# Fifteen shared up-projection blocks instead of thirteen, with four of their gates made in the mixer

## The chip, the core and the metric

One core of a Trainium2 chip runs the whole program. The metric is the device time of one execution in microseconds (us). TensorE (PE) does the matrix products, VectorE (DVE), ScalarE (ACT) and GpSimd (POOL) the elementwise work, and SyncE (SP) issues the transfers between DRAM and the on-chip memory. Each engine takes its instructions in a fixed order and waits at the head of that order for what the next one needs. Results of PE land in eight banks of accumulator memory (PSUM), each 128 x 512 fp32.

## What is computed

One decoder layer on 1024 tokens of width 1024: a mixer (RWKV-7 heads beside a causal convolution, one input and one output projection) and then a gated feed-forward part of hidden width 2816. The change touches the second:

```
h   = rms_norm(x, norm_pre_ffn)
hid = h @ ffn_up                      # 1024 -> 2 x 2816
hid = causal_dwconv(hid, width 3) + b
f   = (gelu(hid[:, :2816]) * hid[:, 2816:]) @ ffn_down
x   = x + rms_norm(f, norm_post_ffn)
```

## The kernel before

**Tiles.** The 1024 tokens are two halves, h0 and h1, of 512. The 2816 hidden columns are FT = 22 blocks of 128; block i has a gate (branch 0) and an up part (branch 1). Every fp32 factor is split into a high and a low part, so one product of a 128x128 weight tile with 512 tokens is three matmuls (high·high, high·low, low·high). One branch of one block for one half is 8 weight tiles, so 24 matmuls of 512 columns, in two weight loads of four tiles each; `weight` loads 256 KB, ACT casts the high part (`wh`) and POOL or DVE subtracts for the low part (`wl`).

**Two ways for a block.** `ffn_pair` makes both branches of one block for one half: 48 matmuls, 96 for both halves. The other way saves products by a Strassen scheme over (two halves of the tokens) x (gate, up) x (two halves of the 1024 inputs): `gates` makes the full gate of h0, which is 24 matmuls, and keeps the partial product after the first four weight tiles (`firsts`); later `shared` gets everything else out of five products of 12 matmuls, from sums of weights (`four_sums`) and sums of activations (`act_sums`). That is 84 matmuls. JOINT blocks go the second way, PLAIN = FT - JOINT the first.

**Order.** The mixer comes first. In its last part PE alternates between the small matmuls of the recurrence, of `conv_norm` and of the other chains, and `ffn_pair` of h0 for the first EARLY blocks, whose results go to DRAM (`early`). The mixer has only two banks, tag `pb`, for these products: each new product takes the bank of the product before the last one and has to wait until `taps` has read that. `taps` is one pass of ACT over the bank, a small ACT copy of two columns, and two passes of DVE (L910, L912, L919). `w_out` for h1 ends the mixer. Then come `gates` for the shared blocks, `ffn_pair` of h1 for the plain ones (with `act_sums` and `weight_sums` interleaved by `beside`), `shared`, and `ffn_down`, a Strassen scheme again, whose weight sums `weight_sums` has left in DRAM (12 sets: four 256 KB loads, four POOL operations, four 256 KB stores each). In the feed-forward part products rotate over six banks. The order of instructions on each engine is set by a scheduler from priorities when the program is built.

In the order of the code before, EARLY = 9, JOINT = 13, PLAIN = 9.

Of the kernel before, what the change touches and what calls it, by code (L numbers as in the profile page):

```python
# [52 lines left out]
EARLY = 9  # L53

JOINT = 13
PLAIN = FT - JOINT

# [43 lines left out]
class Trunk:  # L101
# [99 lines left out]
    def setup(self):  # L201
# [23 lines left out]
        self.lows = self.dp.tile([22, 2, P, 4, P], F32, name="lows")  # L225
        self.sums = self.dp.tile([4, HT, P, 512], F32, name="sums")
# [551 lines left out]
    def w_out(self, h, mixr, co, behind=None):  # L778
# [13 lines left out]

        def evac(ch, pss, post):
# [15 lines left out]
        for ch in range(4):  # L809
# [3 lines left out]
            for k2 in range(KT // 2):  # L813
                wh, wl = self.weight(self.a["w_out"][ch, k2], [P, 2, 256], (self.mix, "ca", "ck") if h else None)
                if ch == 1 and k2 == 0:
                    mark = self.load
# [15 lines left out]
        return mark  # L832


    def setup_ffn(self, ctx):
# [14 lines left out]
                      **{t: cycle([self.wq] * MORE_PAIRS + [self.wp] * PAIRS) for t in ("wh", "wl")}}  # L850
        self.post_ffn = cp.tile([P, D], F32, name="post_ffn")
# [51 lines left out]
    def taps(self, h, i, br, ps, acc):  # L903
# [3 lines left out]
        carry = (self.ecarry if i < EARLY else self.fcarry)[:, br, i]  # L907
# [13 lines left out]
    def ffn_pair(self, h, hs, i, temp, out=None):  # L921
# [10 lines left out]
        self.gated = nc.vector.tensor_tensor(out, gate, accs[1], ALU.mult)  # L932
        return out
# [25 lines left out]
    def gates(self, hs, acts, firsts, side):  # L959
# [9 lines left out]
        for n, i in enumerate(range(PLAIN, FT)):  # L969
# [118 lines left out]
    def weight_sums(self):  # L1088

        nc, a = self.nc, self.a  # L1090
        work = [(lambda r, c, j=j: a["ffn_down"][c, r * HT + j], lambda n, j=j: self.sums[n - 1, j]) for j in range(HT)]
        work.insert(2, (lambda r, c: a["ffn_up"][c * FT + PLAIN, r].rearrange("p k m -> p (k m)"),
                        lambda n: self.usums[n - 1]))
        for src, dst in work:
            b = [self.tp.tile([P, 512], F32, tag="tp", name=self.nm("b")) for _ in range(4)]
# [27 lines left out]
    def ffn_down(self, acts):  # L1123
# [4 lines left out]
        B = lambda r, c: lambda j: self.a["ffn_down"][c, r * HT + j]  # L1128
# [92 lines left out]
    def run(self):  # L1221
# [6 lines left out]
        with ExitStack() as ctx:  # L1228
# [5 lines left out]
            sums = self.weight_sums()  # L1234
            temp = lambda: self.f2p.tile([P, HALF], F32, tag="f2", name=self.nm("acc"))
            act = lambda: self.ap.tile([P, HALF], F32, tag="act", name=self.nm("act"))
            one = [self.ffn_pair(0, h0, i, temp, act()) for i in range(EARLY, PLAIN)]
            both = [[act() for _ in range(JOINT)] for _ in range(2)]
            turn = cycle((True, False))
            self.gates(h0, *both, lambda: self.beside(*[norm] if len(h1) == 0 else [norm, sums] if next(turn) else []))  # L1240
# [9 lines left out]
            for n, i in enumerate(range(PLAIN, FT)):  # L1250
                self.shared(i, S, h1[4:], both[0][n], both[1][n], raws[n % 2 * 4:n % 2 * 4 + 4] if n else None)
            kept = []
            for i in range(0, 8, 2):
# [234 lines left out]
```

## Time and profile before

| | |
|---|---|
| three runs | 1252.01, 1254.13 (median), 1255.34 us |
| the profiled execution | 1257.58 us, of which the span of the profile is 1255.8 us |
| mean granted clock of PE | 0.985 |
| busy, share of the span | DVE 72%, ACT 58%, POOL 40% |
| mixer up to the first up-projection of h0 | 0 to 500 us |
| mixer, recurrence beside early blocks | 500 to 640 us |
| `w_out` for h1 | 640 to 698 us |
| feed-forward part | 698 us to the end; the last matmuls end about 9 us before it (row at 1243.76 us, twelve matmuls in 2.88 us) |

A row of a timeline or of a list of groups gives engine, line of the code, operation, output, input and shape. The duration of a matmul in it runs from its issue to its modelled end, and successive matmuls overlap; so the time that a stream of matmuls takes is read from the distance of their starts, not from the mean duration.

### The profile page before, as it was taken

The page shows a single profiled execution, that of the slowest core. Times are in us where ns is not written, and L with a number is a line of the kernel's source. Part 1 is how long each engine was busy: PE and PEld are TensorE (multiplying, and loading weights), DVE is VectorE, ACT ScalarE, POOL GpSimd, SP SyncE. Part 2 cuts the span into 40 slices and gives each one's busy share as a digit, 9 for nine tenths or more (in the row PEclk, how much of TensorE's full clock was granted, in tenths as well). Part 3 has the DMA queues.
Part 4 walks back from the last instruction along what each step waited for, and adds up shares of the span by engine and source line. Part 5 has one row for each costly group of instructions (what it writes and reads, how often), then busy time and mean ns, then how long its engine had stood idle before and what let it go on. Part 6 is the DMA issues. An engine that isn't in the chain of part 4 may idle for free.

```text
span 1255.8 us, 22979 instructions
## 1 busy us (share of the span) xinstructions
PE 1210.4 (96%) x8424; PEld 988.9 (79%) x8424; DVE 899.8 (72%) x1558; ACT 729.1 (58%) x1515; POOL 507.1 (40%) x447
## 2 busy tenths in 40 slices
PE   5999999999999998999999999999999999999997
PEld 4767777787778876778889888888888888888885
DVE  5285998898669989998640555666656679479667
ACT  7563564565955676466762576876555566554451
POOL 4343330001103331344563399998888850000002
PEclk9999998999999989999999999999999999999999
DMA  7644442333343353222364798894322335336413
GB/s 243 177 131 137 129 135 64 97 128 119 114 128 91 97 178 110 75 80 85 104 186 118 271 323 293 298 315 153 82 74 81 101 134 166 95 117 219 134 52 134
DMA packets 102912, 180.97 MB, mean 144 GB/s; under 512 B 14896, under 2 KB 21424, under 8 KB 102800
## 3 DMA queue, kind: packets, MB, share of 16 engines
q1 hardware_dynamic: 102800, 179.51, 45.6%
q8 instruction: 66, 1.08, 0.4%
q14 instruction: 46, 0.38, 0.1%
HBM read 138.44 MB, written 41.03 MB: 143 GB/s over the span
## 4 chain that ended last, share of the span: by engine, by line
PE 62%; DVE 6%; ACT 2%; issue 1%; DMA 1%; POOL 1%; POOLq 0%; DVEq 0%; ACTq 0%
PE pb L140 27%; PE xs L140 16%; PE pe L140 14%; PE Y L140 2%; PE pc L140 2%; DVE pc L431 2%; DMA pt<-mixd 1%; PE pc L155 1%; PE pe L155 0%; DVE x L1120 0%; DVE m L167 0%; DVE sub L606 0%; DVE nrow L1136 0%; DVE dw L608 0%; DVE t L797 0%
## 5 line engine op out<-in xcount | busy, mean ns | idle before, releaser
L167 POOL TENSOR_TENSOR wl<-wr,wh 128x512 fp32r<-128x512 f32 (+1 forms) x175 | 230.0, 1316 | 219.4 <-ACT wh L167 191.3
L140 PE MATMUL pb<-h,wh 128*128 128x512 f32 (+3 forms) x720 | 230.1, 399 | 2.5 <-ACT wh L167 1.0
L167 ACT CAST wh<-wr 128x512 fp32r<-128x512 f32 (+1 forms) x214 | 131.4, 615 | 131.8 <-issue 42.3
L140 PE MATMUL pb<-f,wh 128*128 128x512 f32 x648 | 205.0, 397 | 2.7 <-ACT wh L167 1.7
L431 DVE SCALAR_TENSOR_TENSOR pc<-c,params,pc 128x512 f32<-128x512 f32 x232 | 174.2, 751 | 8.7 <-ACT pc L428 4.7
L140 PEld LDWEIGHTS pb<-h,wh 128*128 128x128 f32 (+2 forms) x720 | 132.1, 189 | 35.4 <-ACT wh L167 2.7
L140 PE MATMUL pb<-h,wl 128*128 128x512 f32 (+3 forms) x360 | 146.8, 408 | 2.3 <-POOL wl L167 2.1
L140 PEld LDWEIGHTS pb<-f,wh 128*128 128x128 f32 x648 | 121.8, 190 | 28.8 <-ACT wh L167 2.1
L140 PE MATMUL pb<-f,wl 128*128 128x512 f32 x324 | 129.2, 399 | 0.9 <-POOL wl L167 0.9
L162 POOL TENSOR_TENSOR ss<-var,mhalf 128x1 f32<-128x1 f32 x16 | 11.4, 716 | 223.8 <-DVE var L161 223.0
L1076 POOL TENSOR_TENSOR b<-b,b 128x512 f32<-128x512 f32 x72 | 93.3, 1298 | 1.9 <-DMA wr<-ffn_up 0.5
L140 PEld LDWEIGHTS pb<-h,wl 128*128 128x128 f32 (+2 forms) x360 | 67.8, 188 | 20.5 <-POOL wl L167 4.0
L140 PE MATMUL xs<-f,wh 128*128 128x512 f32 x240 | 74.2, 390 | 0.4 <-DVE act L973 0.4
L167 POOL TENSOR_TENSOR wl<-b,wh 128x512 fp32r<-128x512 f32 x48 | 66.6, 1388 | 16.9 <-ACT wh L167 14.9
L140 PEld LDWEIGHTS pb<-f,wl 128*128 128x128 f32 x324 | 61.7, 190 | 14.8 <-POOL wl L167 1.7
L167 ACT CAST wh<-b 128x512 fp32r<-128x512 f32 x48 | 29.7, 618 | 60.0 <-PE pb L140 20.5
L140 PE MATMUL pe<-f,wh 128*128 128x512 f32 x208 | 64.1, 389 | 0.0
L721 POOL TENSOR_TENSOR XG<-r,GE 64x256 f32<-64x256 f32 x30 | 20.5, 683 | 89.3 <-DVE r L740 84.5
L140 PEld LDWEIGHTS xs<-f,wh 128*128 128x128 f32 x240 | 44.9, 188 | 10.0 <-DVE act L973 0.8
L192 ACT CAST wh<-wr 128x512 fp32r<-128x512 f32 (+2 forms) x44 | 26.5, 604 | 44.4 <-PE pb L140 31.2
L167 ACT CAST a<-act 128x512 fp32r<-128x512 f32 x50 | 30.0, 620 | 33.6 <-PE Y L140 19.1
L167 ACT CAST w<-wr 128x512 fp32r<-128x512 f32 x38 | 23.4, 622 | 40.7 <-PE Y L140 20.0
(419 smaller groups left out, 2952.3 us busy)
## 6 DMA issues: line engine op xcount, KB each, us to landing
wr<-ffn_up SPq DMA_DIRECT2D x99, 256.0 KB, 3.2
wr<-w_in SPq DMA_DIRECT2D x80, 256.0 KB, 2.9
b<-ffn_up SPq DMA_DIRECT2D x52, 256.0 KB, 2.7
b<-ffn_down SPq DMA_DIRECT2D x44, 256.0 KB, 4.5
sums<-b SPq DMA_DIRECT2D x44, 256.0 KB, 4.2
wr<-sums SPq DMA_DIRECT2D x44, 256.0 KB, 2.8
lows<-wl SPq DMA_DIRECT2D x40, 256.0 KB, 3.3
wl<-lows SPq DMA_DIRECT2D x40, 256.0 KB, 2.7
```

The source lines that it names most:

```text
L140: return self.nc.tensor.matmul(out, lhsT, rhs, start=start, stop=stop, skip_group_check=skip)
L155: self.nc.tensor.transpose(out, in_, self.con("ident")[:n, :n])
L162: self.nc.gpsimd.tensor_tensor(out, v[:, :n], self.mhalf[:, :n], ALU.pow)
L167: return self.nc.scalar.copy(hi, src), eng.tensor_tensor(lo, src, hi.bitcast(F32), ALU.subtract)
L192: self.nc.scalar.copy(hi, raw)
L431: nc.vector.scalar_tensor_tensor(out, c[:, j:j + HALF], w(j), acc, ALU.mult, ALU.add)
L721: nc.gpsimd.tensor_tensor(x[64:128], R[64:128, gs], w.GE[64:128, c, gs].unsqueeze(2).broadcast_to([64, 4, CH]), ALU.mult)
L1076: sub = lambda o, x, y, op=ALU.subtract: self.nc.gpsimd.tensor_tensor(o, x, y, op)
```

## The change

JOINT becomes 15, PLAIN and EARLY become 7. So that the mixer keeps its supply of matmuls, four of the shared blocks (AHEAD = 4) get their `gates` part there: `ffn_two` joins one such gate with one early block, for the early blocks 2 to 5. The gate and the partial product go to DRAM as one 512 KB row and are loaded back while the first four shared blocks run; shared blocks are taken in the order 4 to 14, then 0 to 3. Four of the twelve sets of weight sums are issued during `w_out` for h1, each behind a given weight load, and eight remain in the feed-forward part. `act_sums`, twelve steps, goes with six of the seven plain blocks instead of with nine. `ffn_down` sees the hidden blocks in another order (`ORDER`); nothing else changes in it.

```diff
-EARLY = 9
-JOINT = 13
+EARLY = 7
+AHEAD = 4
+AT = 2
+SETS = (1, 3, 5, 7)
+JOINT = 15
+ORDER = [*range(PLAIN + AHEAD, FT), *range(PLAIN, PLAIN + AHEAD), *range(PLAIN)]
...
+    def ffn_two(self, hs, n, temp, out, row):
+        nc = self.nc
+        i = PLAIN + n
+        first, gate = row[:, :HALF], row[:, HALF:]
+        accs = [temp() for _ in range(2)]
+        def branch(br, j):
+            ps = self.project(self.a["ffn_up"][br * FT + j], P, hs)
+            self.taps(0, j, br, ps, accs[br])
+        ps = self.bank()
+        self.four(ps, self.weight(self.a["ffn_up"][i, 0], [P, 4, P]), hs[:4], True, True)
+        with self.tc.high_priority():
+            nc.scalar.copy(first, ps)
+        j = n + AT
+        branch(0, j)
+        self.four(ps, self.weight(self.a["ffn_up"][i, 1], [P, 4, P]), hs[4:], False, True)
+        self.taps(0, i, 0, ps, gate)
+        branch(1, j)
+        nc.scalar.activation(gate, gate, AF.Gelu_apprx_tanh)
+        nc.scalar.activation(accs[0], accs[0], AF.Gelu_apprx_tanh)
+        nc.sync.dma_start(self.ahead[n], row)
+        nc.vector.tensor_tensor(out, accs[0], accs[1], ALU.mult)
+        return out
...
-        for n, i in enumerate(range(PLAIN, FT)):
+        for n, i in enumerate(range(PLAIN + AHEAD, FT)):
...
-                self.beside(sums, *[ss] * (2 if i % 3 == 0 else 1))
+                self.beside(*[sums] * (i < PLAIN - 2), *[ss] * (3, 2, 2, 2, 2, 1, 0, 0)[i])
...
-            for n, i in enumerate(range(PLAIN, FT)):
-                self.shared(i, S, h1[4:], both[0][n], both[1][n], raws[n % 2 * 4:n % 2 * 4 + 4] if n else None)
+            for m, n in enumerate([*range(AHEAD, JOINT), *range(AHEAD)]):
+                self.shared(PLAIN + n, S, h1[4:], both[0][n], both[1][n], raws[m % 2 * 4:m % 2 * 4 + 4] if m else None)
+                if m < AHEAD:
+                    with self.tc.issue_after(self.load.ins):
+                        nc.sync.dma_start(both[1][m], self.ahead[m, :, :HALF])
+                        nc.sync.dma_start(both[0][m], self.ahead[m, :, HALF:])
...
+                if AT <= i < AT + AHEAD:
+                    out = self.ffn_two(h0, i - AT, piece, half, self.row("row", 4))
+                else:
+                    out = self.ffn_pair(0, h0, i, piece, half)
...
+            self.sum_tile = lambda: self.tl("pt", [P, 512])
+            self.parts = self.weight_sums()
+            for load, low in (self.marks[i] for i in SETS):
+                with tc.issue_after(load.ins), tc.issue_after(low.ins):
+                    next(self.parts)
```

**PE, between two products in the late mixer.** Before, the end of branch 1 of an early block (`pb_6734`) is followed by branch 0 of the next (`pb_6780`), whose bank is that of the product before:

```order
L140 MATMUL pb_6734<-f_5990,wh_6755 128x512
L140 MATMUL pb_6734<-f_5991,wh_6755 128x512
L140 MATMUL pb_6734<-f_5990,wl_6756 128x512
L140 MATMUL pb_6780<-f_5976,wh_6783 128x512
L140 MATMUL pb_6780<-f_5977,wh_6783 128x512
```

In the changed program this is the end of the gate of the third `ffn_two` (`pb_6699`, the twelve matmuls of its second half) and the start of branch 1 of the early block that goes with it (`pb_6782`). `xs` are small matmuls of the recurrence, `pc` transposes of `conv_norm`:

```order
L146 MATMUL pb_6699<-f_5992,wh_6762 128x512
L146 MATMUL pb_6699<-f_5991,wl_6763 128x512
L146 MATMUL xs_101<-r_7170,l_792_5306 64x64
L146 MATMUL xs_102<-r_7170,l_792_5306 64x64
...
L161 MATMUL pc_6177<-const,t_908_6175 128x128 x4
L146 MATMUL pb_6782<-f_5977,wh_6785 128x512
```

With two banks in rotation `pb_6782` stands in the bank of `pb_6699` itself: opened, then `pb_6719` in the other bank, then closed, then `pb_6782`. Between the two stand eight `xs` and four `pc` rows. The other three `ffn_two` look alike; between the closing matmul and branch 1 stand 16 rows of 32x32 and 16 of 64x64 in the first, 16 of 64x64 and eight of 128x128 in the second, and twelve of 128x128 in the fourth.

**ACT, at the same place of the changed program.** `wh_6785` and `wh_6803` are the two weight halves of `pb_6782`; L918 and L920 are ACT's part of `taps`, first for branch 0 (`pb_6719`), then for the gate (`pb_6699`):

```order
L173 CAST wh_6785<-wr_6783 128x512
L918 ACTIVATE pt_6697<-pb_6719,params 128x512
L920 COPY ecarry<-pb_6719 128x2
L173 CAST wh_6803<-wr_6801 128x512
L918 ACTIVATE row_6696<-pb_6699,params 128x512
L920 COPY ecarry<-pb_6699 128x2
```

The cast of `wh_6803` has moved ahead of the read of the gate's bank, and it takes one of two `wh` buffers, that of the gate's second weight half. On DVE the two passes over `pb_6719` stand ahead of the two over `pb_6699`. In the second `ffn_two` DVE has other work between the two passes over the gate's bank (`pb_6566`): a step of the recurrence (L747) twice, a convolution step (L438) and a step of `finish` (L781):

```order
L927 SCALAR_TENSOR_TENSOR row_6563<-pb_6566,params,row_6563 128x511
L747 TENSOR_TENSOR r_7112<-xs_101,XG_7121 64x256
L438 SCALAR_TENSOR_TENSOR pc_6131<-c_3587,params,pc_6131 128x512
L781 TENSOR_TENSOR mixr_5247<-mixr_5247,pt_3089 128x2x128
L747 TENSOR_TENSOR r_7112<-xs_102,XG_7124 64x256
L927 SCALAR_TENSOR_TENSOR row_6563<-pb_6566,params,row_6563 128x510
```

Before, none to three other operations lie between the two passes over a bank.

**ACT, at the end of the early blocks.** `wh_7018` is the last weight half of the last early block before; `wm` is the first weight tile of `w_out`, and `l_1100` are the casts of the convolution's four outputs for `w_out`:

```order
L167 CAST wm_7343<-wr_7341 128x512
L167 CAST l_1100_7319<-co_4614 128x512
L167 CAST l_1100_7319<-co_4647 128x512
L167 CAST l_1100_7319<-co_6096 128x512
L167 CAST l_1100_7319<-co_6129 128x512
L167 CAST wh_7018<-wr_7016 128x512
L910 ACTIVATE pt_6992<-pb_6955,params 128x512
```

In the changed program the last weight half is `wh_7024`, and the four casts stand some twenty rows behind it:

```order
L173 CAST wh_7006<-wr_7004 128x512
L173 CAST wm_7349<-wr_7347 128x512
L173 CAST wh_7024<-wr_7022 128x512
L918 ACTIVATE pt_6998<-pb_6961,params 128x512
L920 COPY ecarry<-pb_6961 128x2
```

More of the change, by code (lines that the diff above doesn't have):

```diff
@@ L814, in w_out @@
                 wh, wl = self.weight(self.a["w_out"][ch, k2], [P, 2, 256], (self.mix, "ca", "ck") if h else None)
[L815 to L816 removed]
+                self.marks.append((self.load, self.low))
                 for t in range(4):
@@ L1090, in weight_sums @@
         nc, a = self.nc, self.a
-        work = [(lambda r, c, j=j: a["ffn_down"][c, r * HT + j], lambda n, j=j: self.sums[n - 1, j]) for j in range(HT)]
-        work.insert(2, (lambda r, c: a["ffn_up"][c * FT + PLAIN, r].rearrange("p k m -> p (k m)"),
+        work = [(lambda r, c, j=j: a["ffn_down"][c, ORDER[r * HT + j]], lambda n, j=j: self.sums[n - 1, j]) for j in range(HT)]
+        work.insert(2, (lambda r, c: a["ffn_up"][c * FT + PLAIN + AHEAD, r].rearrange("p k m -> p (k m)"),
                         lambda n: self.usums[n - 1]))
         for src, dst in work:
-            b = [self.tp.tile([P, 512], F32, tag="tp", name=self.nm("b")) for _ in range(4)]
+            b = [self.sum_tile() for _ in range(4)]
             for n in range(4):
@@ L1233, in run @@
                                  ("pn", "pn2"), pool=self.h1p)
-            sums = self.weight_sums()
+            sums = self.parts
             temp = lambda: self.f2p.tile([P, HALF], F32, tag="f2", name=self.nm("acc"))
             act = lambda: self.ap.tile([P, HALF], F32, tag="act", name=self.nm("act"))
-            one = [self.ffn_pair(0, h0, i, temp, act()) for i in range(EARLY, PLAIN)]
             both = [[act() for _ in range(JOINT)] for _ in range(2)]
             turn = cycle((True, False))
-            self.gates(h0, *both, lambda: self.beside(*[norm] if len(h1) == 0 else [norm, sums] if next(turn) else []))
+            self.gates(h0, both[0][AHEAD:], both[1][AHEAD:],
+                       lambda: self.beside(*[norm] if len(h1) == 0 else [norm, sums] if next(turn) else []))
             list(norm)
@@ L1409, in mixer @@
                     two = self.row("row", 4)
-                nc.sync.dma_start(self.early[i], self.ffn_pair(0, h0, i, piece, two[:, i % 2 * HALF:(i % 2 + 1) * HALF]))
+                half = two[:, i % 2 * HALF:(i % 2 + 1) * HALF]
+                if AT <= i < AT + AHEAD:
+                    out = self.ffn_two(h0, i - AT, piece, half, self.row("row", 4))
+                else:
+                    out = self.ffn_pair(0, h0, i, piece, half)
+                nc.sync.dma_start(self.early[i], out)
         prepare(4)
         with self.stream("proj"):
-            self.start = self.w_out(1, mixes[1], [sts[1]["co", i] for i in range(4)], W[3].merged)
+            self.w_out(1, mixes[1], [sts[1]["co", i] for i in range(4)], W[3].merged)
+            self.start = self.marks[4][0]
+            self.sum_tile = lambda: self.tl("pt", [P, 512])
[3 more added lines that the diff above has]
+                    next(self.parts)
         return h0
```

27 lines of the change are left out of this document (14 added, 13 removed).

## The prediction

> **What bounds the kernel.** I read the page first: busy shares, the row of slices, the chain that ended last. Then busy time by stage.
>
> ```profile
> span 1255.8 us, 22979 instructions
> ...
> PE 1210.4 (96%) x8424; PEld 988.9 (79%) x8424; DVE 899.8 (72%) x1558; ACT 729.1 (58%) x1515; POOL 507.1 (40%) x447
> ...
> PE   5999999999999998999999999999999999999997
> ```
>
> ```profile
> 500.00:640.00 140.00, 136.85 (x1244) 109.53 (x1245) 118.16 (x189) 86.84 (x179) 63.34 (x51) 0.98 0.29 87
> 640.00:698.00 58.00, 57.64 (x435) 55.42 (x434) 7.62 (x11) 19.27 (x51) 25.99 (x20) 1.00 0.51 146
> 698.00:1246.00 548.00, 547.62 (x2430) 453.25 (x2431) 373.17 (x595) 320.89 (x659) 287.55 (x227) 1.00 0.53 171
> ```
>
> After the span of a window the columns are PE, weight loads, DVE, ACT, POOL, then PE's granted clock and the DMA. PE is never idle from 698 us on (547.62 of 548), nearly never in `w_out` (57.64 of 58), and in the late mixer for 3.15 of 140 us. So there is nothing to win by moving work about: in these stages the time falls only with PE's own work, and every new wait of PE is added in full.
>
> **Fewer matmuls: 5.4 us less.** A shared block costs 84 matmuls of 512 columns instead of 96, so two more save 24. In the mixer it is even: before 9 blocks of 48, after 7 of 48 and 4 gates of 24, 432 both times. In the feed-forward part gates fall from 312 to 264, plain blocks from 432 to 336, and shared ones rise from 780 to 900. The price is not the mean duration of a group, since matmuls overlap:
>
> ```profile
> L140 PE MATMUL xs<-f,wh 128*128 128x512 f32 x240 | 74.2, 390 | 0.4 <-DVE act L973 0.4
> ```
>
> ```profile
> 709.75 2.72 PE pe L140 x12
> 712.47 2.72 PE xs L140 x12
> ```
>
> The first says 390 ns for one; the chain of waits has twelve in 2.72 us, 0.227 us each. 24 x 0.227 = **5.4 us**, 0.43%; the 390 ns would have made 9.4 of it.
>
> **A new wait in the mixer: 8.7 us more.** The mixer has two `pb` banks. Today a product takes the bank of the last but one, with 24 matmuls (5.4 us) between. In `ffn_two` branch 1 takes the bank of the gate that was closed just before it, and PE stands until `taps` has read that bank. How long that takes is in the trace:
>
> ```profile
> 601.75 0.39 PE L140 MATMUL pb<-f,wl 128*128 128x512 f32 x1
> 602.64 0.78 ACT L910 ACTIVATE pt<-pb,params 128x512 f32<-128x512 f32 x1
> 603.50 1.53 DVE L919 SCALAR_TENSOR_TENSOR pt<-pb,params,pt 128x511 f32<-128x511 f32 x2 [0.53 <-ACT ecarry L912]
> ...
> 610.59 0.39 PE L140 MATMUL pb<-f,wl 128*128 128x512 f32 x1
> 611.36 0.77 ACT L910 ACTIVATE pt<-pb,params 128x512 f32<-128x512 f32 x1
> 613.48 0.74 DVE L919 SCALAR_TENSOR_TENSOR pt<-pb,params,pt 128x510 f32<-128x510 f32 x1
> ...
> 577.26 0.39 PE L140 MATMUL pb<-f,wl 128*128 128x512 f32 x1
> 578.03 0.77 ACT L910 ACTIVATE pt<-pb,params 128x512 f32<-128x512 f32 x1
> 580.63 0.74 DVE L919 SCALAR_TENSOR_TENSOR pt<-pb,params,pt 128x511 f32<-128x511 f32 x1
> 582.54 0.74 DVE L919 SCALAR_TENSOR_TENSOR pt<-pb,params,pt 128x510 f32<-128x510 f32 x1
> ```
>
> From the end of the last matmul to the end of the second DVE pass: 2.9 us (602.14 to 605.03), 3.2 (610.98 to 614.22), and 5.6 (577.65 to 583.28) where DVE had convolution steps in between. Today nobody waits for it. I start from the middle row, 3.2 us, and add the weight cast that now stands ahead of the gate's read on ACT and can start only when the gate's last matmul has released its buffer: 0.62 us (row at 602.00 below). That is 3.9 us for the first, third and fourth `ffn_two`. In the second, DVE has four other operations between the two passes over the gate; I take 5.0, towards the slow row. Together 16.7 us.
>
> Beside it runs what the order puts between:
>
> ```profile
> 602.00 0.62 ACT L167 CAST wh<-wr 128x512 fp32r<-128x512 f32 x1 [2.05 <-issue]
> ```
>
> ```profile
> 470.34 0.95 PE L140 MATMUL xs<-r,l 128*64 128x64 f32 x16 [0.24 <-ACT r L697]
> 473.00 0.27 PE L140 MATMUL xs<-XG,l 64*64 64x64 f32 x1
> ...
> 473.93 0.22 PE L140 MATMUL Y<-r,l 64*64 64x64 f32 x1
> ...
> 619.48 0.60 PE L155 MATMUL pc<-const,co 128*128 128x128 f32 x4
> 620.38 0.60 PE L155 MATMUL pe<-const,mixr 128*128 128x128 f32 x4
> 620.81 1.06 PE L140 MATMUL pe<-gd,lora 96*128 96x128 f32 x8
> ```
>
> ```profile
> 540.59 0.62 PE pe L140 x32
> ```
>
> A row of the order that is not fp32r is two instructions in the trace. A group of 16 `xs` and `Y` rows takes 1.15 us (473.00 to 474.15), 16 rows of 32x32 0.6, four transposes 0.60, eight matmuls of the output gate with their transposes 1.5 (620.38 to 621.87), eight `xs` rows 0.95. So 1.75, 2.65, 1.55 and 2.1 us lie in the four places, 8.0 together. PE stands 16.7 - 8.0 = **8.7 us**. With every release as fast as the fastest row it is 4 x 2.9 - 8.0 = 3.6, with every one as slow as the slowest 4 x 5.6 - 8.0 = 14.4. Behind the waiting matmul on PE are the recurrence's next steps, so they come later too; nothing but PE waits for them, and their work isn't lost. One recurrence step also has lost the large matmuls between its two halves and waits for ACT's copy of `xs`: 0.8 us, my estimate from one copy and the latency to it (0.4 after a matmul, as above), between 0 and 1.5.
>
> **What the wait does to the clock: 1.7 us more.** The late mixer already has one stop of PE:
>
> ```profile
> 631.97 2.19 ACT L167 CAST l<-co 128x512 fp32r<-128x512 f32 x4
> 634.05 0.63 ACT L167 CAST wh<-wr 128x512 fp32r<-128x512 f32 x1
> 634.74 0.73 PE L140 MATMUL pb<-f,wh 128*128 128x512 f32 x2 [1.70 <-ACT wh L167]
> 636.39 0.50 PE L140 MATMUL pb<-f,wl 128*128 128x512 f32 x1 [0.92 <-POOL wl L167]
> ```
>
> ```profile
> 635.00:640.00 5.00, 4.08 (x12) 2.88 (x12) 3.30 (x4) 3.13 (x6) 4.27 (x3) 0.70 0.42 127
> 640.00:645.00 5.00, 5.00 (x41) 4.91 (x40) 2.34 (x3) 3.78 (x8) 4.08 (x3) 0.96 0.86 237
> ```
>
> After it the granted clock is 0.70 and 0.96 over two windows of 5 us: 1.5 + 0.2 = 1.7 us lost besides the 2.6 us of idle time. A wait of two or three microseconds next to small matmuls may do the same, up to four times (0 to 6.8 us). Groups of small matmuls as long as 2 us lie all through this stage at a clock of 0.98, so I count one, 1.7 us.
>
> **The old stop goes: 4.3 us less.** That stop came from ACT's order: the last weight's cast stood behind four casts of the convolution's outputs (2.19 us). After the change these stand behind all weight casts of the early blocks. What is late next there is `w_out`'s own second half, which needs them; some fifty matmuls of 256 columns stand ahead of it. I take the whole 2.6 + 1.7 = **4.3 us**; the other end is 0.
>
> **What I cost at nothing or little.** The four sets of weight sums in `w_out`: 16 POOL operations of 1.30 us,
>
> ```profile
> L1076 POOL TENSOR_TENSOR b<-b,b 128x512 f32<-128x512 f32 x72 | 93.3, 1298 | 1.9 <-DMA wr<-ffn_up 0.5
> ```
>
> ```profile
> 800.00:850.00 50.00, 50.00 (x222) 41.44 (x221) 32.96 (x50) 38.81 (x81) 46.82 (x38) 1.00 0.89 302
> ```
>
> add 20.8 us to POOL's 25.99 of 58, and 32 transfers (8.4 MB) to a DMA busy for 0.51. SP issues them in its order, so a store that waits for POOL holds the weight loads behind it. The plain stage carries the same load today (POOL 46.82 of 50, DMA 0.89) and PE is full, 50.00. Cost 0; if a load comes late, up to 3. The four rows of gates to DRAM and back are 4 MB, written in the late mixer at 0.29 of the DMA and read long before they are used. Each store waits on SP for the gate's gelu with weight loads behind it, as the stores of the early blocks do today; PE waits for none of those loads there. Cost 0.
>
> `act_sums` is tighter. It has 44 ACT operations of 0.6 us, 26 us, now mostly beside five plain blocks (5 x 48 x 0.227 = 54 us) instead of nine. ACT has 38.81 of 50 us there, 8.4 for one block with 1.33 steps of 2.2 us; with 2.2 steps it is 10.3 of 10.9 us. Weight casts have priority; cost **0.5 us**, between 0 and 4.
>
> **Sum.** -5.4 + 8.7 + 0.8 + 1.7 - 4.3 + 0.5 = **+2.0 us**. It changes the profiled execution of 1257.58 us to 1259.6. That execution is 3.45 us above the median of the runs, 1254.13, so against the median I forecast **1256 us**. A measurement of this kernel can tell about 0.3%, 3.8 us, from no change; so this is no change.
>
> **Rivals.**
> *The clock falls at each new wait* (slower). Price 4 x 1.7 = 6.8 instead of 1.7, sum +7.1, **1261 us**. For it: 0.70 after one short stop, and the four places hold 4 to 5 us of small matmuls and waiting. Against it: small groups alone don't do it. It decides from the second slow window on; three make +5.4. [...]
> *The banks come free early* (faster). DVE and ACT have more time when PE waits; releases like the fastest row make 3.6 us, at full clock: -5.4 + 3.6 - 4.3 = -6.1, **1248 us**. For it: two of the releases here are at 2.9 and 3.2. Against it: the cast ahead of the read, and DVE busy for 118 of 140 us.
> *ACT or the DMA becomes the bound* in the plain stage or in `w_out` (slower): +4 and +3 at worst, +2.0 + 3.5 or + 3, or both: **1259 to 1262 us**.
> That the saving isn't there I don't count: the order has 24 fewer matmuls of 512 columns.
>
> **Chances.** The forecast 0.38 (its own range 1251 to 1258), clock 0.26, late casts or loads 0.08, early banks 0.28. So faster 0.28, same 0.38, slower 0.34. The range goes from a little below the early banks, 1246, to the clock's case with slow releases, 1265.
>
> **What would show it.** In the late mixer: four waits of PE for `pb` released by DVE L927, 1 to 3 us each, none at 634 us; the granted clock after each; a stage that is 5 to 8 us longer. From `w_out` on: PE full, and a feed-forward part 5.4 us shorter. PE waiting for `wh` in the plain stage, or for `wm` in `w_out`, would make the last rival right; waits below 1 us, the second.

## The result, and the profile after

| | median | lowest to highest | runs |
|---|---|---|---|
| before | 1253.66 us | 1252.01 to 1257.67 | 10 |
| after | 1260.38 us | 1257.51 to 1263.15 | 10 |

The ratio is 1.0052, with a 95% interval of 1.0042 to 1.0062: the change costs 6.7 us. The time lies in the range that was given, 4.4 us above the forecast. The forecast itself, no change within 0.3%, did not come true: the change makes the kernel slower by more than that.

The two profiled executions don't show this: 1257.58 us before, 1257.83 after. The one of before lies at the top of its range, the one of after near the bottom. The first matmul on `f`, the input of h0's up-projections, is at 500.38 us before and at 494.78 after, and up to there both programs do the same; the granted clock of that stretch is 0.97 and 0.99. So the traces have to be compared stage by stage, from marks on PE: that first matmul on `f`, the first matmul of `w_out` on `wm`, and the first matmul of the feed-forward part that waits for ACT's last pass of `w_out`. Page and windows of after, with the same columns as those of before:

```profile
span 1256.1 us, 22928 instructions
...
PE 1199.9 (96%) x8400; PEld 980.0 (78%) x8400; DVE 904.7 (72%) x1566; ACT 730.7 (58%) x1519; POOL 513.5 (41%) x453
```

```profile
494.78:633.27 138.49, 133.25 (x1240) 107.00 (x1241) 110.08 (x181) 83.79 (x174) 58.31 (x49) 1.00 0.32 98
633.27:699.66 66.39, 60.82 (x438) 57.30 (x436) 14.06 (x16) 25.61 (x62) 49.97 (x39) 0.97 0.77 257
699.66:1246.00 546.34, 543.07 (x2404) 448.02 (x2405) 379.83 (x605) 318.76 (x656) 274.62 (x217) 1.00 0.48 155
```

The same marks in the trace of before:

```profile
500.38:640.34 139.96, 137.19 (x1244) 109.75 (x1245) 117.78 (x188) 86.80 (x179) 63.34 (x51) 0.98 0.30 88
640.34:697.89 57.55, 57.19 (x433) 55.06 (x431) 7.51 (x11) 18.93 (x50) 25.99 (x20) 1.00 0.50 144
697.89:1246.00 548.11, 547.73 (x2430) 453.36 (x2431) 373.28 (x595) 320.89 (x659) 287.55 (x227) 1.00 0.53 171
```

PE is busy 10.5 us less, 1199.9 for 1210.4, and yet the time is longer. The late mixer takes 138.49 us instead of 139.96, `w_out` **66.39 instead of 57.55**, and from the third mark to the end of the span 556.4 instead of 557.9. From the first mark to the third that is +7.4, behind it -1.5.

I add up PE's idle time in the same two parts, from the bracketed figures of its timeline: before 3.0 us up to the third mark and 0.4 behind it, after **10.6 and 3.2**. The waits of after, in three places. The late mixer (start, duration, then what was waited for):

```profile
528.45 0.73 PE L146 MATMUL pb<-f,wh 128*128 128x512 f32 x2 [1.51 <-DVE pt L927]
554.83 0.74 PE L146 MATMUL pb<-f,wh 128*128 128x512 f32 x2 [1.31 <-DVE pt L927]
578.08 0.27 PE L146 MATMUL xs<-XG,l 64*64 64x64 f32 x1 [0.66 <-ACT XG L726]
580.06 0.74 PE L146 MATMUL pb<-f,wh 128*128 128x512 f32 x2 [0.83 <-DVE pt L927]
```

Where these stand is found by counting. In PE's order the products on `f` follow the first mark in runs of so many matmuls of 512 columns to one bank (tiles in order; a tile named twice is a gate, before and behind its break):

```
24 24 24 24 | 12 pb_6434  24 pb_6454  12 pb_6434  24 pb_6517 | 12 pb_6566  24 pb_6586  12 pb_6566  24 pb_6649 | ...
```

The three waits on `pt` come after 108, 180 and 252 matmuls, which is the start of **branch 0** (`pb_6454`, `pb_6586` and the like) of the first three joined blocks, not of branch 1. The releaser fits: DVE writes the gate to `row`, and only the branches of an early block to `pt`.

The banks are not what the text ahead of the prediction says, either. In the program as built the gates of all four joined blocks (`pb_6434`, `pb_6566`, `pb_6699`, `pb_6831`) stand in bank 6 and both branches of each in bank 5; `pb_6782` is in the bank of `pb_6719`, not in that of `pb_6699`. The trace agrees. These are the last matmul of the third gate and the first of the branch 1 behind it:

```profile
591.66 0.39 PE L146 MATMUL pb<-f,wl 128*128 128x512 f32 x1
...
593.01 0.70 PE L146 MATMUL pb<-f,wh 128*128 128x512 f32 x2
```

Branch 1 opens 0.96 us after the gate has closed, without a wait, and the fastest release among the prediction's rows took 2.9 us. The start of `w_out`, and its end, with ACT's casts of the first weights of the feed-forward part:

```profile
635.84 0.63 PE L161 MATMUL pc<-const,t 128*128 128x128 f32 x4 [0.86 <-DVE t L454]
639.22 1.82 PE L146 MATMUL xs<-wm,l 128*128 128x256 f32 x13 [0.84 <-POOL wm L173]
646.57 0.66 PE L146 MATMUL pb<-wm,l 128*128 128x256 f32 x2 [1.07 <-DVE l L173]
684.81 0.73 PE L146 MATMUL pe<-f,wh 128*128 128x512 f32 x2 [1.88 <-ACT pe L812]
```

```profile
674.00 0.62 ACT L173 CAST wh<-wr 128x512 fp32r<-128x512 f32 x1 [9.06 <-DMA wr<-ffn_up]
674.53 1.14 ACT L173 CAST wm<-wr 128x512 fp32r<-128x512 f32 x2
680.22 0.62 ACT L173 CAST wh<-wr 128x512 fp32r<-128x512 f32 x1 [4.55 <-DMA wr<-ffn_up]
683.24 0.62 ACT L173 CAST wh<-wr 128x512 fp32r<-128x512 f32 x1 [2.40 <-DMA wr<-ffn_up]
683.77 0.37 ACT L812 ACTIVATE pe<-pe 128x256 f32<-128x256 f32 x1
```

PE first waits for the convolution's outputs (`t`, `l`) and a split weight (`wm`). At the end ACT has sat in front of casts whose weights had not landed, the last until 683.24, and reads the bank `pe`, for which PE waits, only behind them. And in the plain stage:

```profile
809.43 0.70 PE L146 MATMUL pb<-f,wh 128*128 128x512 f32 x2 [1.21 <-DVE acc L927]
```

with 0.61 us for POOL's `wl` at 840.75 and 0.96 for ACT at 855.16.

### The profile page after: what moved, and what is told of

The parts are those of the page before. It is cut to its first block, busy times and chain, and to the rows that moved or that the text cites. A ratio compares the mean times of both kernels' runs of the same rounds, so it can differ in the third digit from the quotient of the medians.

```text
span 1256.1 us, 22928 instructions
## 1 busy us (share of the span) xinstructions
PE 1199.9 (96%) x8400; PEld 980.0 (78%) x8400; DVE 904.7 (72%) x1566; ACT 730.7 (58%) x1519; POOL 513.5 (41%) x453
## 4 chain that ended last, share of the span: by engine, by line
PE 53%; DVE 10%; DMA 3%; ACT 3%; POOL 2%; issue 2%; SPq 0%; POOLq 0%; DVEq 0%; ACTq 0%
PE pb L146 22%; PE xs L146 13%; PE pe L146 13%; DVE pc L438 3%; PE Y L146 2%; PE pc L146 2%; DMA wr<-ffn_up 1%; DMA pt<-mixd 1%; DMA wr<-w_out 1%; DVE pt L927 1%; DVE sub L613 1%; PE pc L161 1%; DMA pt<-ffn_up 1%; POOL wl L173 1%; DVE dw L615 0%
## 5 line engine op out<-in xcount | busy, mean ns | idle before, releaser
L173 POOL TENSOR_TENSOR wl<-wr,wh 128x512 fp32r<-128x512 f32 (+1 forms) x165 | 216.3, 1314 | 211.3 <-ACT wh L173 182.0
L146 PE MATMUL pb<-f,wh 128*128 128x512 f32 x624 | 196.5, 394 | 6.0 <-DVE pt L927 3.7
L173 ACT CAST wh<-wr 128x512 fp32r<-128x512 f32 (+1 forms) x204 | 125.1, 614 | 119.7 <-PE pb L146 34.9
L438 DVE SCALAR_TENSOR_TENSOR pc<-c,params,pc 128x512 f32<-128x512 f32 x232 | 174.1, 750 | 7.3 <-ACT pc L435 3.3
L146 PEld LDWEIGHTS pb<-f,wh 128*128 128x128 f32 x624 | 115.5, 188 | 31.3 <-DVE pt L927 4.0
L173 POOL TENSOR_TENSOR wl<-b,wh 128x512 fp32r<-128x512 f32 x56 | 76.0, 1358 | 23.1 <-ACT wh L173 22.9
L1110 POOL TENSOR_TENSOR b<-b,b 128x512 f32<-128x512 f32 x60 | 77.6, 1293 | 1.5
L146 PE MATMUL xs<-f,wh 128*128 128x512 f32 x200 | 62.1, 391 | 1.4 <-ACT pb L1104 1.0
L173 ACT CAST a<-act 128x512 fp32r<-128x512 f32 x62 | 37.0, 620 | 40.1 <-PE Y L146 18.9
L173 DVE TENSOR_TENSOR a<-act,a 128x512 fp32r<-128x512 f32 x62 | 42.3, 699 | 19.9 <-ACT a L173 19.4
L146 PEld LDWEIGHTS pe<-f,wh 128*128 128x128 f32 x224 | 42.0, 188 | 10.7 <-ACT pe L812 2.1
```

The source lines that it names most:

```text
L146: return self.nc.tensor.matmul(out, lhsT, rhs, start=start, stop=stop, skip_group_check=skip)
L173: return self.nc.scalar.copy(hi, src), eng.tensor_tensor(lo, src, hi.bitcast(F32), ALU.subtract)
L438: nc.vector.scalar_tensor_tensor(out, c[:, j:j + HALF], w(j), acc, ALU.mult, ALU.add)
L1110: sub = lambda o, x, y, op=ALU.subtract: self.nc.gpsimd.tensor_tensor(o, x, y, op)
```

## The experiments

Three rounds for the first four, five for the others, each against the kernel before on the same chip. "Waits" are PE's, from each one's trace: from the first mark to the third, and from there to the end.

| | median us | ratio to before [95%] | waits us |
|---|---|---|---|
| after | 1260.38 | 1.0052 [1.0042, 1.0062] | 10.6 + 3.2 |
| 1 sums made late | 1274.90 | 1.0157 [1.0140, 1.0173] | 5.6 + 14.2 |
| 2 sums only | 1255.35 | 1.0005 [0.9986, 1.0023] | 3.0 + 4.8 |
| 3 gate in one | 1255.50 | 1.0011 [0.9995, 1.0027] | 3.7 + 3.9 |
| 4 ACT spread | 1259.62 | 1.0032 [1.0018, 1.0047] | 9.1 + 1.4 |
| 5 other bank | 1262.79 | 1.0064 [1.0052, 1.0076] | 11.2 + 3.2 |
| 6 at one | 1260.82 | 1.0052 [1.0036, 1.0068] | 5.4 + 4.4 |
| 7 all three | 1260.40 | 1.0037 [1.0023, 1.0051] | 5.4 + 5.1 |
| 8 no sums | 1255.01 | 1.0004 [0.9994, 1.0015] | 6.9 + 1.3 |
| 9 copy between | 1255.36 | 1.0021 [1.0010, 1.0032] | 6.8 + 1.6 |
| 10 POOL stores | 1264.10 | 1.0090 [1.0076, 1.0103] | 6.3 + 7.1 |
| 11 three sets | 1254.79 | 1.0002 [0.9992, 1.0012] | 8.3 + 1.4 |
| 12 two sets | 1253.07 | 0.9985 [0.9972, 0.9998] | 6.0 + 1.0 |

### 1. The sums made late

```diff
-            for load, low in (self.marks[i] for i in SETS):
-                with tc.issue_after(load.ins), tc.issue_after(low.ins):
-                    next(self.parts)
...
+                if m in (1, 4, 7, 10):
+                    self.sum_eng = nc.vector
+                    with self.tc.issue_after(self.load.ins), self.tc.issue_after(self.low.ins):
+                        next(sums)
```

> The changed kernel with one part undone: no weight sums beside w_out; the four sets are made among the shared blocks instead, on DVE, one behind the weight loads of every third block. Theory W (w_out takes 66.4 us instead of 57.6 because the four sets' loads, POOL work and stores stand in the way of its weights and of the next stage's): w_out to the first gate comes back to 57 to 60 us, and the time falls from 1260.4 by 6 to 9 us, to 1251.5 to 1254.5, less what DVE cannot hide among the shared blocks. Theory O (the loss there comes from the new order at the end of the early blocks, where the four casts and splits of the convolution's outputs stand later): w_out still takes 63 to 66 us, and the time stays between 1258 and 1262.

`w_out` took 60.09 us, close to what theory W wants, and the whole 14.5 us more, as neither theory does. PE's order is that of the changed kernel from end to end, and the four casts stand as late; only the sums are gone from `w_out`. With them it took 66.39 us, and 64.85 to 66.76 in experiments 4 and 5: beside this order the sums are worth **5 to 7 us of `w_out`**. PE's timeline among the shared blocks:

```profile
885.12 1.06 PE L147 MATMUL xs<-f,wh 128*128 128x512 f32 x2 [3.07 <-DVE acc L1068]
931.73 0.70 PE L147 MATMUL pb<-f,wh 128*128 128x512 f32 x2 [3.96 <-DVE acc L1068]
978.45 1.19 PE L147 MATMUL xs<-f,wh 128*128 128x512 f32 x2 [4.06 <-DVE acc L1068]
```

```profile
874.19 2.38 DVE L1111 TENSOR_TENSOR b<-b,b 128x512 f32<-128x512 f32 x2 [2.84 <-DMA b<-ffn_down]
```

DVE stood at the head of its order waiting for the loads of a set, and the additions that free PE's banks (L1068) stood behind. The place that this experiment chose for the sums has its own price, so it tells of `w_out` only, and not of the whole time.

### 2. The sums alone, in the kernel before

```diff
+SETS = (1, 3, 5, 7)
...
+            self.sum_tile = lambda: self.tl("pt", [P, 512])
+            self.parts = self.weight_sums()
+            for load, low in (self.marks[i] for i in SETS):
+                with tc.issue_after(load.ins), tc.issue_after(low.ins):
+                    next(self.parts)
```

> The kernel before (13, 9 and 9 blocks) with nothing added but the four sets of weight sums beside w_out. Theory W: w_out grows from 57.6 us to 64 to 67 us, and the time goes from 1253.7 to 1259 to 1262. Theory O: w_out stays within 2 us of 57.6 and the time within 2 us of 1253.7.

`w_out` stayed at 57.53 us and the time within 1 us. So theory W falls in the form that I gave it: the sums do not make `w_out` long by themselves. But PE, and DVE with it, waits just behind it:

```profile
703.47 1.22 PE L141 MATMUL xs<-f,wh 128*128 128x512 f32 x2 [4.76 <-DVE act L975]
```

```profile
702.72 1.29 DVE L975 COPY act<-xs 128x512 f32<-128x512 f32 x2 [5.03 <-DMA mixd<-t]
```

`mixd<-t` is the last transfer of `w_out`; in the trace of before the same wait of PE is 0.38 us. This trace is of the longest of the ten runs, 1262.71 us, and the median shows no loss, so 4.8 us is not the usual price here.

### 3. The gate in one run

```diff
-        self.four(ps, self.weight(self.a["ffn_up"][i, 0], [P, 4, P]), hs[:4], True, True)
+        self.four(ps, self.weight(self.a["ffn_up"][i, 0], [P, 4, P]), hs[:4], True, False)
+        self.four(ps, self.weight(self.a["ffn_up"][i, 1], [P, 4, P]), hs[4:], False, True)
         with self.tc.high_priority():
             nc.scalar.copy(first, ps)
+        self.taps(0, i, 0, ps, gate)
         j = n + AT
         branch(0, j)
-        self.four(ps, self.weight(self.a["ffn_up"][i, 1], [P, 4, P]), hs[4:], False, True)
-        self.taps(0, i, 0, ps, gate)
         branch(1, j)
```

> The changed kernel, but ffn_two makes its gate in one run of 24 matmuls and then the two branches, so that no product is opened in a bank, left and closed again, and every bank is that of the product before the last one, as in the kernel before. The copy kept as the partial product is taken of the whole product, so the four blocks' outputs differ from the reference; the instructions are the same in number and kind. Theory B (the waits for the banks cost what their rows show, 3.7 us in all): those rows go, the late mixer is 3 to 4 us shorter, and the time falls from 1260.4 to 1256 to 1258. Rival (the recurrence sets the pace there, and PE would wait for it instead): the rows go, the late mixer stays within 1 us, time 1259.5 to 1261. The forecast's price of 8.7 us would give 1251.7.

1.0011 instead of 1.0052: the time falls as theory B said, to just below its bounds. But more than the bank waits went. The order on ACT at the end of the early blocks became that of before, with its old stop (the first two rows below), and `w_out` took 57.52 us with all four sets in it:

```profile
634.35 0.73 PE L146 MATMUL pb<-f,wh 128*128 128x512 f32 x2 [1.72 <-ACT wh L173]
636.00 0.50 PE L146 MATMUL pb<-f,wl 128*128 128x512 f32 x1 [0.92 <-POOL wl L173]
695.91 0.73 PE L146 MATMUL pb<-f,wh 128*128 128x512 f32 x2 [0.36 <-ACT pb L812]
701.35 0.73 PE L146 MATMUL xs<-f,wh 128*128 128x512 f32 x2 [2.42 <-DVE act L1007]
```

So the 66 us are not of the sums alone (experiment 2) and not of the bank waits alone: the split gate also moves the end of the early blocks, and the sums fall into what that leaves. The wait for `act` is there again, 2.42 us.

### 4. The activation sums spread

```diff
-                self.beside(*[sums] * (i < PLAIN - 2), *[ss] * (3, 2, 2, 2, 2, 1, 0, 0)[i])
+                self.beside(*[sums] * (i < PLAIN - 2), *[ss] * (2, 2, 2, 2, 2, 1, 1, 0)[i])
```

> The changed kernel, with the twelve steps of the activation sums spread as 2, 2, 2, 2, 2, 1, 1 and 0 beside the plain blocks instead of 3, 2, 2, 2, 2, 1, 0 and 0. Theory A (the squeezed activation sums make ACT and DVE late in the plain stage, which gave up 3 to 4 of the 5.4 us that fewer matmuls save): the time falls by 1 to 3 us, to 1257.5 to 1259.5. Rival (it is not the spread of these steps that costs there): 1260 to 1261.

The waits of the feed-forward part fall from 3.2 to 1.4 us. Those ahead of it are 9.1 us instead of 10.6, though nothing was changed there: the first wait for a bank, 1.51 us in the trace of after, is missing in this one. It comes and goes with the execution (the trace of experiment 1, with the same order of PE, doesn't have it either). The median is 0.8 us lower; against the kernel before on its own chip the ratio is 0.0020 lower, 2.5 us. The intervals touch, so the time alone supports theory A weakly, the waits plainly.

### 5. Branch 1 in the bank of branch 0

```diff
-            ps = self.project(self.a["ffn_up"][br * FT + j], P, hs)
-            self.taps(0, j, br, ps, accs[br])
+            for half in range(2):
+                self.four(other, self.weight(self.a["ffn_up"][br * FT + j, half], [P, 4, P]),
+                          hs[half * 4:half * 4 + 4], half == 0, half == 1)
+            self.taps(0, j, br, other, accs[br])
         ps = self.bank()
+        other = self.bank()
```

> The changed kernel, with branch 1 of the four joined blocks in the bank of branch 0 instead of in that of the gate: that bank was closed twelve matmuls (2.7 us) earlier, so taps has that much longer to read it. The order on ACT at the end of the early blocks stays that of the changed kernel (the four casts of the convolution's outputs still stand behind the last early block). Theory B (the waits for the bank are what their rows show, three of 0.83 to 1.51 us, 3.7 us in all): the three rows before branch 1 go, and the time falls by 3 to 4 us, from 1260.4 to 1256.5 to 1257.5. Rival (the recurrence is behind by then and PE meets the time again as a wait for it): the rows go, others of the same sum come, time within 1 us of 1260.4.

Nothing went:

```profile
532.70 0.73 PE L146 MATMUL pb<-f,wh 128*128 128x512 f32 x2 [1.52 <-DVE pt L927]
560.67 0.74 PE L146 MATMUL pb<-f,wh 128*128 128x512 f32 x2 [1.32 <-DVE pt L927]
585.87 0.73 PE L146 MATMUL pb<-f,wh 128*128 128x512 f32 x2 [0.84 <-DVE pt L927]
```

The same three waits, to 0.01 us. And nothing could go. Branch 1 stood in the bank of branch 0 already, so the edit moves no product: with the buffer numbers left out, the two programs have the same instructions in the same order on every engine, in the same banks. So this run tests neither theory B nor its rival. It is a second measurement of the changed kernel, on another chip (ratio 1.0064 for 1.0052), and shows how far two traces of one program differ: the wait for `pe` is 3.75 us for 1.88.

I had still taken the three rows for waits at branch 1; only then did I count matmuls and find them at branch 0. There the arithmetic is plain. Two banks, and the gate holds one of them from its first half to its second. Branch 0 gets the other, which the branch 1 before it has just closed; between the two lie only the twelve matmuls of 512 columns of the gate's first half, 2.7 us, where before there were always 24, 5.4 us. Branch 1 follows branch 0 in that same bank, again with twelve between. Three of these eight openings wait in the trace of after; the short distance makes a wait possible, not certain.

### 6. The joined blocks one earlier

```diff
-AT = 2
+AT = 1
```

> The changed kernel, with the four joined blocks at the early blocks 1 to 4 instead of 2 to 5, nothing else. The bank waits of the joined blocks stay possible, but the order on ACT at the end becomes that of the kernel before: first weight tile of w_out, the four casts of the convolution's outputs, then the last weight half of the last early block. Theory O (that order, together with the sums that then fall into a late w_out, costs the 5.5 us of waits seen from 630 to 700 us, against 3.0 before): the waits after 630 us come down to about 3.0, the old stop of 2.6 us before the last early product is back, w_out to the first gate comes to 57 to 58 us, and the time falls by 2 to 4 us, to 1256.5 to 1258.5. Rival (the weight sums alone make w_out long): it stays at 63 to 66 us, time 1260 to 1261.

The first half of theory O holds: `w_out` 57.52 us, and 10.6 us of waits become 5.4. The time doesn't fall. Behind `w_out` PE waits for `act` again, 2.83 us, and the clock is 0.66 for 5 us after it:

```profile
705.07 1.22 PE L146 MATMUL xs<-f,wh 128*128 128x512 f32 x2 [2.83 <-DVE act L1007]
```

```profile
705.00:710.00 5.00, 4.93 (x15) 3.94 (x16) 2.67 (x6) 0.56 (x2) 0.00 (x0) 0.66 0.88 293
```

With the 1.7 us that the clock loses there this is 4.5 us, most of the 5.2 that the waits ahead gave up. A `w_out` that ends earlier meets a `mixd` that doesn't.

### 7. The three edits together

Experiments 4, 5 and 6 in one kernel; since 5 moves nothing, it is 4 and 6 together.

> The three edits together in the changed kernel: branch 1 in the bank of branch 0, the joined blocks at 1 to 4, and the activation sums spread as 2, 2, 2, 2, 2, 1, 1, 0. If bank waits (3.7 us), the order at the end (2.5 us) and the squeezed activation sums (1.8 us) are the causes and add up: 1260.4 less 8.0, so 1252 to 1254, the time of the kernel before or 1 us below it. If they are one and the same delay seen in three places: 1255 to 1257.

They don't add up, and the trace shows where. PE, DVE, and SP's queue, which issues the transfers:

```profile
705.59 1.22 PE L146 MATMUL xs<-f,wh 128*128 128x512 f32 x2 [4.18 <-DVE act L1010]
```

```profile
698.06 0.69 DVE L806 TENSOR_TENSOR t<-pb,po 128x512 f32<-128x512 f32 x1 [0.74 <-PE pb L146]
...
704.84 1.29 DVE L1010 COPY act<-xs 128x512 f32<-128x512 f32 x2 [3.72 <-DMA mixd<-t]
```

```profile
695.89 1.70 SPq L1137 DMA_DIRECT2D sums<-pt  x2
698.51 0.33 SPq L190 DMA_DIRECT2D wr<-ffn_up  x1
699.76 1.69 SPq L1137 DMA_DIRECT2D sums<-pt  x2
701.54 0.94 SPq L814 DMA_DIRECT2D mixd<-t  x2
```

`t` is ready at 698.75 (698.06 + 0.69), but its transfer is issued at 701.54, behind the last stores of sums, which wait for POOL. In the trace of after it goes out at 698.62, with no such stores just ahead, because `w_out` is late there itself.

### 8. No sums beside `w_out`

Experiment 7 without the four sets; what would read them reads other sums of the same size. The diff leaves those readers out.

```diff
-            for load, low in (self.marks[i] for i in SETS):
-                with tc.issue_after(load.ins), tc.issue_after(low.ins):
-                    next(self.parts)
...
-        for src, dst in work:
+        for src, dst in work[len(SETS):]:
```

> The kernel with the three edits, but the four sets of weight sums beside w_out aren't made at all; what would read them reads the sums of other columns, in equal number and size, so the outputs differ from the reference. What is left of the feed-forward part is unchanged. Theory W in its small form (the sums cost DMA time at the end of w_out, so the transfer that the normalization waits for lands late, 2 to 5 us of PE's time at the first gates): 2 to 5 us below the kernel with the sums. Rival (the sums are free there, as I forecast): within 1 us of it.

1255.01 us against 1260.40, the ratio 1.0004 against 1.0037: the four sets cost **4 to 5 us** in this kernel (2 to 6 by the two intervals), and the wait for `act` is 0.34 us instead of 4.18. I had them at 0. The other traces agree: that wait is 2.42 to 4.76 us wherever SP issues all four sets beside a `w_out` of 57.5 us (2, 3, 6, 7), and 0.33 to 0.42 us where the sums are absent (before, 1, 8), fewer (11, 12), or `w_out` is itself late (after, 4, 5, 9). Where the order is that of before without joined blocks, in experiment 2, they cost between -1.8 and +2.9 us. Why the same wait costs less there in the median I can't say.

### 9. The gate in one run, the copy between its halves

```diff
         j = n + AT
-        branch(0, j)
         self.four(ps, self.weight(self.a["ffn_up"][i, 1], [P, 4, P]), hs[4:], False, True)
         self.taps(0, i, 0, ps, gate)
+        branch(0, j)
         branch(1, j)
```

> The changed kernel, with the gate of a joined block made in one run of 24 matmuls as in the third experiment, but with the partial copy taken correctly between its halves: the second half waits for that copy, and the banks alternate product by product as in the kernel before. The waits of the late mixer moved when branch 1 took another bank, no fewer in sum, because they stand at the start of branch 0: its bank is that of the branch 1 before it, and only the twelve matmuls of the gate's first half lie between. Theory B2 (it is that short distance that costs): the waits on DVE's second pass go, a wait for the ACT copy of at most 1 us takes their place at each of the four, the waits of the late mixer add up to 3 to 6 us, and the order at its end is that of the kernel before; time 1256 to 1258.5, against 1255.5 with the copy misplaced. Rival (joining itself costs, wherever the copy stands): 1260 to 1262.

1255.36 us, ratio 1.0021 instead of 1.0052. Two waits are left at the joined blocks, 2.3 us together:

```profile
559.13 0.73 PE L146 MATMUL pb<-f,wh 128*128 128x512 f32 x2 [1.01 <-DVE pt L927]
582.39 0.74 PE L146 MATMUL pb<-f,wh 128*128 128x512 f32 x2 [1.30 <-ACT row L957]
```

The second is the wait for the copy, before the second half of the third gate. The first is the old one: in the second block the scheduler has put half of branch 0 between the halves of the gate, so that its bank again has only twelve matmuls of distance. Moving two lines of the change gives back 3.9 us of the 6.7 (0.0031 of 1254), give or take 1.9. The banks are not where it comes from. Of the waits of after only the first, 1.51 us, has no counterpart here, and the traces of experiments 11 and 12, with the same order of PE in the mixer, have it again: 1.60 and 1.00 us for banks and 1.31 for the copy in 11, 3.9 together, against 3.65 in after. So theory B2 had the time and not the mechanism. What changed is the end of the early blocks. The convolution's casts, first here and then in after:

```profile
629.40 2.19 ACT L173 CAST l<-co 128x512 fp32r<-128x512 f32 x4
```

```profile
643.47 2.18 ACT L173 CAST l<-co 128x512 fp32r<-128x512 f32 x4
```

They stand early again, PE's waits for the convolution's outputs are gone, and `w_out` takes 62.65 us.

### 10. The stores issued by POOL

```diff
-                nc.sync.dma_start(dst(n), b[t])
+                self.out_queue.dma_start(dst(n), b[t])
...
+            self.out_queue = nc.gpsimd
```

> The kernel with the three edits, but POOL issues the sixteen stores of the four sets of sums beside w_out, not SP. In the trace of the three edits the last four of them stand on SP ahead of the transfer that the normalization waits for (mixd): they wait for POOL, it waits behind them, and PE waits 4.18 us for what follows, at the first gates. Theory W2 (this place on SP is the price of the sums): that wait falls to 0.4 us, and the time falls by 2 to 5 us, to 1255.5 to 1258.5. Rival (the transfers of the sums fill the DMA engines, or POOL is late): the wait stays above 2 us, time within 1 us of 1260.4; worse by 1 to 4 us if issuing on POOL delays the weights that it splits.

The transfer of `t` now starts at 697.84 us, and the wait for `act` falls to 1.64. But in this trace POOL pays 0.56 us for nearly every store, in its own order, and its weights come late:

```profile
705.76 0.50 PE L146 MATMUL pb<-f,wl 128*128 128x512 f32 x1 [2.60 <-POOL wl L173]
711.40 0.73 PE L146 MATMUL xs<-f,wh 128*128 128x512 f32 x2 [1.64 <-DVE act L1011]
```

The place on SP was part of that wait, as theory W2 says, but the wait does not fall to 0.4, and moving the stores is no remedy: the ratio is 0.0053 above that of experiment 7, 6.6 us. The rival's last case, POOL late with the weights that it splits, came true, beyond its 4 us.

### 11 and 12. Fewer sets beside `w_out`

Experiment 9 with the spread of experiment 4, and three or two sets instead of four. The diff is of the second; the first has `(1, 3, 5)` and sums beside all plain blocks but the last.

```diff
-SETS = (1, 3, 5, 7)
+SETS = (1, 3)
...
-                self.beside(*[sums] * (i < PLAIN - 2), *[ss] * (3, 2, 2, 2, 2, 1, 0, 0)[i])
+                self.beside(sums, *[ss] * (2, 2, 2, 2, 2, 1, 1, 0)[i])
```

> The changed kernel with three edits: the gate in one run with the copy between its halves (1255.4 by itself), the activation sums spread as 2, 2, 2, 2, 2, 1, 1, 0 (1.2 us of waits in the plain stage to be had), and three sets of weight sums beside w_out instead of four, the ninth set then beside the sixth plain block. The last four stores of sums no longer stand on SP between the weight loads of the first gates and the transfer that the normalization waits for. If each of the sets beside w_out costs its share of the 4 to 5 us that leaving out all four was worth (and the ninth set is free in the plain stage): 1252 to 1254, the time of the kernel before or a little below it. Rival (POOL, over 85 per cent busy in the plain stage, has no room for a ninth set there): waits for POOL's low parts or at the first shared block, 1255 to 1258.

> The same with two sets beside w_out and ten in the feed-forward part, one beside each plain block. Theory (what the sums cost beside w_out falls set by set, and the plain stage takes them): 1250.5 to 1252.5, below the kernel before. Rival (the plain stage is full: POOL's low parts become late there, or the last sets end behind its last block): slower than with three sets by 1 to 4 us.

With three sets the time is that of before, with two 0.15% below it, by an interval that just leaves out 1. Both medians lie a little above what was expected (1252 to 1254, and 1250.5 to 1252.5). The windows with two sets, cut at the same marks:

```profile
497.08:635.94 138.86, 133.17 (x1234) 107.00 (x1235) 117.34 (x186) 87.99 (x182) 59.70 (x50) 0.99 0.32 98
635.94:695.74 59.80, 59.44 (x444) 56.90 (x442) 7.51 (x11) 20.29 (x53) 37.36 (x30) 1.00 0.66 215
695.74:1246.00 550.26, 543.95 (x2408) 448.79 (x2408) 382.43 (x616) 317.84 (x657) 286.13 (x227) 1.00 0.49 163
```

PE is busy for 59.44 of the 59.80 us of `w_out`, and the plain stage takes the two more sets: 1.0 us of waits behind the third mark. What stands between the -5.4 us of the matmuls and the -1.9 measured (0.0015 of 1254) are the waits up to the third mark, 6.0 us instead of 3.0, of which 2.6 are still for banks and 1.3 for a copy, and 0.6 more behind it: -5.4 + 3.0 + 0.6 = -1.8.

## Why the range held, and where the steps did not

The forecast was +2.0 us on the profiled execution, and +6.7 was measured between the medians. That is outside the forecast's own range, 1251 to 1258, and on the slower side, which had a chance of 0.34. The wide range held it partly by luck: errors of both signs stood in the sum. Step by step:

- **Fewer matmuls, -5.4.** Elapsed from the third mark to the end, less the waits, is 557.5 us before and 553.2 after: -4.3 in one trace each, about right.
- **A new wait, +8.7, four times, at branch 1.** The size was too large and the place wrong: three waits, 3.65 us, at branch 0. At branch 1 there is no wait of PE. The step that failed is the rotation that I assumed: I put branch 1 into the bank of the gate, closed just before, and priced that bank's release; as built, branch 1 stands in the bank of branch 0, and the short distances are those of bank 5. The low end, 3.6 us, is close to what was measured, but by luck and not by its argument.
- **The recurrence, +0.8.** 0.66, for the reason given.
- **The clock, +1.7.** The granted clock stays at 1.00 over the whole late mixer: 0 after the bank waits. It falls in `w_out` instead, to 0.67 between 645 and 650 us, 1.6 us, where three waits (0.23, 0.23 and 1.07 us) come within 2.5 us.
- **The old stop, -4.3.** It is gone, as forecast, and so is its clock loss. I had named what is late next, `w_out`'s second half, and priced it at nothing. The waits from 635 to 647 us add up to 3.2 us (the three rows shown and two of 0.23). With the clock all of it is given back. Experiment 6, which brings the old order back, has the old stop, 1.5 us there, and none of these. The sums have a share in them: experiment 1, with the casts as late but no sums, keeps one, of 1.57 us. And the 1.7 us of clock in the price are not a constant of that stop: experiments 2 and 3 have the same two waits (1.67 and 0.93, 1.72 and 0.92) at a granted clock of 1.00.
- **The weight sums, 0 with an upper end of 3.** The largest error: 4 to 5 us by experiment 8, and 5 to 7 us of `w_out` by experiment 1. I had judged by POOL's and the DMA's busy shares, and by the plain stage, which carries the same load with PE full. But the plain stage has no transfer on which the next stage hangs, and `w_out` ends in one. The order on SP decided, as I had written of the weight loads, and not of `mixd`. In the trace of after the same sums show as weight loads that land late (the 9.06 us of ACT).
- **`act_sums`, +0.5, up to 4.** 1.8 us of waits go with the spread of experiment 4. Named and mis-sized, within its bounds.

Among the rivals, "the clock falls at each new wait" gave 1261 us, the closest single number, and by its mechanism it was wrong: no wait for a bank of the late mixer lowered the clock; the three of 0.83 to 1.51 us, some 25 us apart, left it at 1.00. The third rival, late loads in `w_out` and ACT in the plain stage, 1259 to 1262 us, had most of the mechanism, at a chance of 0.08.

From the first mark to the end the two traces differ by 5.9 us. PE's waits add 10.4 of it (13.8 instead of 3.4), and the clock nothing (1.6 us lost in `w_out`, 1.7 no longer lost at the old stop). That leaves -4.5, near the -5.4 of the matmuls. So the waits are what the change costs; how they divide among the causes isn't settled to a microsecond, since the edits move one another's waits. The experiments give 3.9 us for the order at the end of the early blocks (9), 2.5 for the spread (4) and 4 to 5 for the sums (8), each give or take some 2 us. The waits for banks, 3.65 us by their rows, have no experiment of their own: experiment 3 takes them away together with that order. Experiment 12, with the order, the spread and half of the sums changed, is 8.4 us below the changed kernel by the ratios.

## What to carry to other kernels

When a product holds a bank while others go on, list for each bank what closes it and what opens it next, with the number of matmuls between, and take the banks from the program as built, not from the order of the program text. And see that an experiment's edit changes the built program before reading its time. Work put beside a stage for its idle engines was not free here, where the transfer that ends the stage stood behind it in a queue (PE waited 4.18 us with the sums, 0.34 without, experiments 7 and 8): look for the last transfer of the stage and for what was issued just ahead. And compare two traces by stage from common marks, with the waits added up, before believing that two equal totals mean no change.

## What the runs showed of the hardware

Two single stops of PE, 1.88 us in after and 2.37 in experiment 9, left the granted clock at 1.00 in the next window of 5 us. After 2.42 us (experiment 3) it was 0.75 and 0.90 in two windows, after 2.60 (experiment 10) and 2.83 (experiment 6) 0.66 in one, and after 4.18 (experiment 7) 0.91, 0.50 and 0.91 in three. The window of 0.50:

```profile
705.00:710.00 5.00, 4.41 (x10) 3.47 (x11) 2.69 (x5) 0.00 (x0) 0.00 (x0) 0.50 0.75 262
```

What is missing to a clock of 1.00, times 5 us, is some 1.7 us for each of the first three and 3.4 us for the last: so much, by this estimate, did these stops cost beyond the wait itself. The clock fell at shorter waits that came close together, too (in after to 0.67, with 0.23, 0.23 and 1.07 us between 644 and 647 us; in before to 0.70, with 1.70 and 0.92 us), but not always: in experiment 3 1.72 and 0.92 us left it at 1.00.
